# Asking for the last weight pieces earlier and splitting three of them on POOL, at the turn from gate products to position steps

## The chip, the cores and the metric

The program runs on one core of one Trainium2 chip. The metric is the device time of one execution in microseconds (us); less is better. The engines are named as in the profile: PE (TensorE matmul) with PEld (its weight loads), DVE (VectorE), ACT (ScalarE), POOL (GpSimd) and SP (SyncE, which here only issues DMAs).

## The reference

Two sequences, one of 2048 and one of 512 positions with 1024 channels, pass through the same trunk, all in float32:

```python
for layer in (attention, fourier):
    h = rmsnorm(x, g)
    # attention: o = banded grouped-query attention with sinks (|i-j| <= 128)
    # fourier:   f = Re(2-D FFT over (positions, 256 channels of a group)) of h
    x = x + (mixer(h) * silu(h @ w_gate)) @ w_out
y = rmsnorm(x, final_norm)
```

Only the second half of the Fourier layer matters here: the gate product `h @ w_gate`, the FFT over positions, the product with the gate, and the output product with `fourier_w_out`.

## The kernel before, in words

Every float32 product is made of three matmuls (`matmul3`, L92 to L94). Each operand is split into an upper part, rounded by an ACT cast, and a lower part, the difference, which an elementwise subtraction makes (`t[:, 1] = src - t[:, 0]`). L92 multiplies upper by upper, L93 upper of the left operand by lower of the right one, L94 lower by upper. So a weight piece is of use to L92 and L94 when ACT has cast it, and to L93 only when its lower part is there too.

`fourier_phase` runs first over ten pairs of 128-row tiles. For each pair `gates` makes the gate product by a scheme of sums: accumulators `W`, `Z` (two PSUM banks tagged `acc`) and `X`. `X` is made in four steps, `x_step(0)` to `x_step(3)`; each uses one 512 KB piece of the block B21 of the gate weights, and calls `more()`, which requests the next piece from DRAM (`b<-b21d`, L830). There are 40 pieces, two ahead at the start, so in the last pair `x_step(0)` requests the 39th piece and `x_step(1)` the 40th, which `x_step(3)` uses. Between the products, `hook(0)` to `hook(6)` run what the caller hands in.

For the last pair these hooks hold the way over to the second half. `f_load(k)` requests one of eight 512 KB pieces of the output weight (`w32f<-in_w_fout_dram`, L1118). `f_split(k)` makes two split tiles of it (`wo`, numbers 2k and 2k+1): ACT casts (L1124) and DVE subtracts (L1125). `position(...)` makes the FFT over positions: `gs` (or `gp`) parts by ACT L1027 and DVE L1028, matmuls into `As` and `Bs`, then ACT L1044 and L1048, DVE L1049, L1050 and the product with the gate rows `s2`, DVE L1052. `split_T` turns the result on PE (`tru`, L729), splits it by ACT L735 and DVE L736 into `tTu`. `finish` loads the residual rows (`x<-x1d`, L1063), makes two output halves of 24 matmuls each (`fo<-wo,tTu`), half 0 with `wo` 0 to 7 and half 1 with `wo` 8 to 15, adds them (DVE L1069), normalises (ACT L744, POOL L87, DVE L1081) and stores (L1082).

In the last pair the hooks run position 1 of the short sequence (`first`, two tiles, rows 2049 and 2051). After `gates` come positions 0 and 2 of it (`new`), then pieces 6 and 7 of the output weight, the splits of pieces 4 to 7, `finish` of the two tiles of `first`, and then the sixteen positions of the long sequence.

The text's order is not the order on the engines. A layer below records all operations, and orders them on each engine by a list scheduler; buffers come from pools (`left` has 20 places of 4 KB per partition, `xtile` four), and an operation that takes a place waits for the last use of it. Inside one engine's queue the order is fixed when the program is built, and a DMA whose wait is not over holds back all that follow on the same queue. `after(a, b)` adds an edge that keeps `a` behind `b` in the order, without a wait of its own. `tc.keep_in_program_order` keeps the ACT casts of `f_split` in the text's order.

Of the kernel before, what the change touches and what calls it, by code (L numbers as in the profile page):

```python
# [13 lines left out]
ALU = mybir.AluOpType  # L14
# [25 lines left out]
def f32(ap):  # L40
    return ap.bitcast(F32)
# [3 lines left out]
def encoder(  # L45
# [3 lines left out]
    PE, ACT, DVE, POOL, SP = nc.tensor, nc.scalar, nc.vector, nc.gpsimd, nc.sync  # L49
# [16 lines left out]
    x1d = dram.tile([T, D], F32, name="x1d")  # L66
# [8 lines left out]
    def bank(name):  # L75
        return psum.tile([P, 512], F32, tag="bank", name=name)

    def xtile(shape, dtype, name):
        return xp.tile(shape, dtype, align_bytes=LINE, tag="x", bufs=4, name=name)
# [10 lines left out]
    def matmul3(out, a, b, start, stop, more=False):  # L90

        PE.matmul(out, a[0], b[0], start=start, stop=False, skip_group_check=more)  # L92
        PE.matmul(out, a[0], b[1], start=False, stop=False, skip_group_check=more)  # L93
        PE.matmul(out, a[1], b[0], start=False, stop=stop, skip_group_check=more)  # L94
# [32 lines left out]
    def after(ins, anchor):  # L127

        if anchor is not None:
            tc.add_manual_dep(ins.ins, anchor.ins.name, ISSUE, reason="issue order")  # L130
# [565 lines left out]
    def fourier_phase(tail):  # L696
        with ExitStack() as es:
# [7 lines left out]
            def left(shape, dtype, name):  # L705
                return fp.tile(shape, dtype, align_bytes=LINE, tag="L", bufs=20, name=name)

            def right(shape, dtype, name):
                return zp.tile(shape, dtype, align_bytes=LINE, tag="R", bufs=16, name=name)
# [107 lines left out]
            def prod(out, a, b, ks, first):  # L817

                for k in ks:
                    cs = slice(k * P, (k + 1) * P)  # L820
                    matmul3(out, (a[0][:, cs], a[1][:, cs]), b[k], first and k == 0, k == 3, not first)
# [3 lines left out]
            def more():  # L825

                k = len(b21)
                if k < 4 * len(pairs):
                    t = right([P, 2, 512], F32R, f"b21_{k}")
                    SP.dma_start(f32(t), f32(b21d[k % 4]))  # L830
                    b21.append((t[:, 0], t[:, 1]))

            def gates(pr, hooks):

                n, A, S = pr.n, pr.A, pr.S
                W = psum2.tile([P, 512], F32, tag="acc", name=f"W{n}")
                Z = psum2.tile([P, 512], F32, tag="acc", name=f"Z{n}")
                X = bank(f"X{n}")

                def x_step(k):  # L840
                    prod(X, A[0, 1], b21[4 * n : 4 * n + 4], (k,), True)
                    more()

                def silu(c, i, half):
                    th = main.tile([P, 512], F32, tag="xr", bufs=3, name=f"gt{pr.ts[i]}_{half}")
                    ACT.activation(th, c, AF.Tanh, scale=0.5)
                    DVE.scalar_tensor_tensor(th, th, 1.0, c, ALU.add, ALU.mult)
                    t = pr.ts[i]
                    dst, t0 = (s2d[0], t) if t < SEQ // P else (s2d[1], t - SEQ // P)
                    POOL.dma_start(dst[t0 * P : (t0 + 1) * P, half * 512 : half * 512 + 512], th)  # L850

                def hook(i):
                    for h in hooks.get(i, ()):
                        h()

                four = range(4)
                c = xtile([P, 2, 512], F32, f"c{n}")
                c11, c22 = c[:, 0], c[:, 1]
                prod(W, A[0, 0], wg["B11"], four, True)
                ACT.copy(c11, W)  # L860
                hook(0)
                x_step(0)
                prod(Z, S[1], wg["T1"], four, True)
                ACT.copy(c22, Z)
                hook(1)
                prod(W, S[2], wg["T2"], four, False)
                c12 = fp.tile([P, 512], F32, tag="c12", bufs=1, name=f"c12_{n}")
                ACT.copy(c12, W)
                hook(2)
                x_step(1)  # L870
                prod(Z, S[4], wg["B22"], four, False)
                DVE.tensor_tensor(c12, c12, Z, ALU.add)
                silu(c12, 0, 1)
                hook(3)
                x_step(2)
                prod(W, S[3], wg["T3"], four, False)
                DVE.tensor_tensor(c22, c22, W, ALU.add)
                silu(c22, 1, 1)
                hook(4)
                x_step(3)  # L880
                DVE.tensor_tensor(c11, c11, X, ALU.add)
                silu(c11, 0, 0)
                hook(5)
                prod(W, A[1, 1], wg["N4"], four, False)
                silu(W, 1, 0)
                hook(6)
# [29 lines left out]
            def x_tile(name):  # L916
                return xtile([P, D], F32, name)

            order = [[16, 17, 18, 19]] + [[a, a + 4, a + 8, a + 12] for a in range(4)]
            pairs = [Pair(2 * gi + i // 2, tiles[i : i + 2]) for gi, tiles in enumerate(order) for i in (0, 2)]  # L920
# [3 lines left out]
            for i, s in enumerate(tail):  # L924
# [3 lines left out]
                if 1 <= i < 9:  # L928
                    w, k = split_steps[i - 1]
# [38 lines left out]
            pr = pairs[0]  # L968
# [23 lines left out]
            def rows(ap, r):  # L992
                return bass.AP(ap.tensor, ap.offset + r[0] * D, [[r[1] * D, P], [1, D]])
# [61 lines left out]
            def finish(uT, r, last=False):  # L1055
                r0 = r[0]
                dst, off = (y_prompt, 0) if r0 < SEQ else (y_sample, SEQ)
                out = rows(dst, (r0 - off, r[1]))
                if last:
                    ss = main.tile([P, 8], F32, tag="ss", bufs=2, name="ssl")  # L1060
                    junk = fp.tile([P, 512], F32, tag="c12", bufs=1, name="jkl").bitcast(BF16)
                x2 = x_tile(f"x2_{r0}")
                SP.dma_start(x2, rows(x1d, r))  # L1063
                for half in range(2):
                    ps = psum2.tile([P, 512], F32, tag="acc", name=f"fo{r0}_{half}")
                    for k in range(KD):
                        matmul3(ps, uT[k], wo[half * KD + k], k == 0, k == KD - 1)
                    xs = x2[:, half * 512 : half * 512 + 512]
                    DVE.tensor_tensor(xs, xs, ps, ALU.add)  # L1069
                    if last:  # L1070
                        ACT.activation(junk[:, :512], xs, AF.Square, accum_out=ss[:, half : half + 1])
                if last:
                    DVE.tensor_tensor(ss[:, 0:1], ss[:, 0:1], ss[:, 1:2], ALU.add)
                    inv = inv_rms(ss, 1, "invl")
                    for half in range(2):
                        hs = slice(half * 512, half * 512 + 512)
                        DVE.scalar_tensor_tensor(x2[:, hs], x2[:, hs], inv[:, 0:1], gfb[:, hs], ALU.mult, ALU.mult)
                        (SP, ACT)[half].dma_start(out[:, hs], x2[:, hs])
                    return
                inv = sumsq(x2, f"f{r0}")  # L1080
                DVE.scalar_tensor_tensor(x2, x2, inv[:, 0:1], gfb, ALU.mult, ALU.mult)  # L1081
                SP.dma_start(out, x2)  # L1082
# [28 lines left out]
                return name, 4 * k1, gl[0], gl[1] if len(gl) > 1 else None, tiles, (s2s, tb)  # L1111

            POOL.dma_start(mir, mirror)
            first, early, wo, w32f = [], [], [], []

            def f_load(k):
                w32f.append(left([P, 2, 512], F32, f"w32f{k}"))
                SP.dma_start(w32f[k].rearrange("p k c -> p (k c)"), w_fout[k // 4, k % 4])  # L1118

            def f_split(k):  # L1120
                for kk in range(2):
                    t = left([P, 2, 512], F32R, f"wo{2 * k + kk}")
                    src = w32f[k][:, kk]
                    tc.keep_in_program_order(ACT.copy(t[:, 0], src))  # L1124
                    DVE.tensor_tensor(t[:, 1], src, f32(t[:, 0]), ALU.subtract)  # L1125
                    wo.append((t[:, 0], t[:, 1]))

            def turn_first(i):
                u, r = first[i]
                pend.append((split_T(u, f"u{r[0]}", r[2] is not None), r))  # L1130
# [5 lines left out]
                2: [lambda: f_load(2), lambda: early.append(sample(2, (1,), (left,), (xtile,), left))],  # L1136
                3: [lambda: first.extend(position(*one)), lambda: f_load(3)],
                4: [lambda: f_split(0), lambda: f_split(1)],
                5: [lambda: turn_first(0), lambda: f_split(2), lambda: f_load(4)],
                6: [lambda: turn_first(1), lambda: f_split(3), lambda: f_load(5)],  # L1140
            })
            new = [t for p in early for t in position(*p)]
            for k in (6, 7):
                f_load(k)
            for k in range(4, 8):
                f_split(k)
            finish(*pend.pop(0))
            new = [(split_T(u, f"u{r[0]}", r[2] is not None), r) for u, r in new]
# [6 lines left out]
            for i, l in enumerate((w0, w2)):  # L1155
                for a in range(3):
                    t = zt(f"ev{a}_{i}")
# [31 lines left out]
            for a in range(4):  # L1189
                for i, l in enumerate((pc, qs)):  # L1190
# [3 lines left out]
                    t = zt(f"od{a}_{i}")  # L1194
# [127 lines left out]
```

## Time and profile before

| | us |
|---|---|
| three runs | 1663.11, 1664.00, 1667.96 |
| their median | 1664.00 |
| the profiled execution | 1665.56 |
| its span on the core | 1663.8 |
| PE busy in the span | 1640.0 (99%) |
| DVE, ACT, POOL busy | 1172.5, 873.8, 382.3 |
| granted TensorE clock, mean | 0.998 |

The profile's page lists busy time by engine, the span in slices, DMA queues, the chain that ended last, groups of instructions and DMA issues. Behind it stand answers of the trace: who waited for whom, the instructions in order of time, busy time by stretch. Times in them are us from the start of the span. A matmul of 512 columns is shown with 0.39 us, but the next one starts 0.23 us after it, since matmuls overlap; a PE that is shown busy may be far from its best. An arrow, as in `[1.94 <-DMA b<-b21d]`, gives the idle time before an instruction and what ended it. "SPq" is SP's queue of DMA issues.

### The profile page before, as it was taken

The numbers are of one execution on the slowest core, as the hardware profiler recorded it, in microseconds if no ns is written. First come the engines' busy times: TensorE is split into PE (matmuls) and PEld (weight loads), VectorE is DVE, ScalarE is ACT, GpSimd is POOL, SyncE is SP. The second block draws the span as 40 slices with busy tenths as digits, with TensorE's granted clock in tenths as the row PEclk, the third lists the DMA queues.
The fourth block names the chain that finished last, engine by engine and source line by source line (L and its number), as shares of the span: only waits on it lengthen the run. The fifth ranks groups of instructions, "written<-read, shape, count | busy, mean of one in ns | idle before, by whom it ended". The sixth has DMA issues, their size and how long they took to land.

```text
span 1663.8 us, 25654 instructions
## 1 busy us (share of the span) xinstructions
PE 1640.0 (99%) x8987; PEld 1410.4 (85%) x8987; DVE 1172.5 (70%) x2810; ACT 873.8 (53%) x1998; POOL 382.3 (23%) x536
## 2 busy tenths in 40 slices
PE   9999999999999999999999999999999999999997
PEld 7888788888898888988888888888888887888886
DVE  5787665888548886478874688768676769888553
ACT  6788644676236674256752466555554545342321
POOL 2465642112402113121122211221111111101000
PEclk9999999999999999999999999999999999999999
DMA  7486886454864456754549644556556578553331
GB/s 276 162 303 232 286 329 227 160 194 156 289 227 164 159 190 221 249 206 155 189 146 329 231 158 158 225 197 230 184 199 234 184 247 319 165 190 125 113 127 51
DMA packets 90252, 340.49 MB, mean 205 GB/s; under 512 B 11099, under 2 KB 21339, under 8 KB 72716
## 3 DMA queue, kind: packets, MB, share of 16 engines
q1 hardware_dynamic: 71676, 261.50, 46.0%
q0 software_dynamic: 18160, 76.56, 11.8%
q8 instruction: 72, 1.18, 0.3%
q10 hardware_dynamic: 288, 0.79, 0.1%
q14 instruction: 56, 0.46, 0.1%
HBM read 263.28 MB, written 75.53 MB: 204 GB/s over the span
## 4 chain that ended last, share of the span: by engine, by line
PE 82%; DVE 5%; ACT 5%; DMA 4%; issue 2%; POOL 1%; SPq 0%; DVEq 0%; POOLq 0%; ACTq 0%
PE spt L404 5%; PE av L457 5%; PE pt L443 5%; PE qp L92 4%; PE qp L94 4%; PE qp L93 4%; PE gp L92 4%; PE gp L94 4%; PE gp L93 4%; PE op L92 4%; PE op L94 3%; PE op L93 3%; PE fo L93 3%; PE fo L94 3%; PE fo L92 3%
## 5 line engine op out<-in xcount | busy, mean ns | idle before, releaser
L420 ACT ACTIVATE S<-S 128x385 f32<-128x385 f32 (+1 forms) x320 | 191.0, 597 | 46.8 <-DVE S L416 45.3
L444 ACT CAST pts<-pt 128x384 fp32r<-128x384 f32 (+1 forms) x320 | 144.2, 453 | 109.1 <-PE pt L443 104.5
L445 DVE TENSOR_TENSOR pts<-pt,pts 128x384 fp32r<-128x384 f32 (+1 forms) x320 | 168.3, 527 | 43.9 <-ACT pts L444 40.7
L416 DVE CUSTOM_DVE_ANT_0 S<-spt,b 128x385 f32<-128x385 f32 (+1 forms) x320 | 168.8, 528 | 34.7 <-PE spt L404 31.6
L404 PE MATMUL spt<-kwin,qab 128*128 128x384 f32 (+1 forms) x640 | 157.2, 327 | 1.1 <-DVE S L416 1.1
L476 POOL TENSOR_TENSOR o<-o,s 128x256 f32<-128x256 f32 x75 | 55.4, 739 | 437.7 <-DVE o L474 437.4
L443 PE MATMUL pt<-ident,S 128*128 128x128 f32 x896 | 150.6, 273 | 0.7 <-ACT S L429 0.6
L404 PEld LDWEIGHTS spt<-kwin,qab 128*128 128x128 f32 x640 | 118.2, 188 | 26.9 <-DVE S L416 1.7
L457 PEld LDWEIGHTS av<-pts,v 128*128 128x128 f32 x896 | 126.4, 189 | 14.0 <-DVE qab L353 1.6
L92 PE MATMUL gp<-h,wg 128*128 128x512 f32 x320 | 137.8, 431 | 0.0
L92 PE MATMUL qp<-h,wq 128*128 128x512 f32 x320 | 136.9, 428 | 0.8 <-DVE v L318 0.8
L457 PE MATMUL av<-pts,v 128*128 128x256 f32 x896 | 136.1, 285 | 1.4 <-DVE qab L353 1.1
L92 PE MATMUL op<-wo,uT 128*128 128x512 f32 x320 | 126.5, 397 | 1.5 <-ACT invb L165 0.8
L92 PE MATMUL fo<-wo,tTu 128*128 128x512 f32 x320 | 125.8, 393 | 1.3 <-ACT wo L1124 1.3
L443 PEld LDWEIGHTS pt<-ident,S 128*128 128x128 f32 x896 | 113.6, 140 | 15.7 <-DVE pts L445 3.2
L94 PE MATMUL qp<-h,wq 128*128 128x512 f32 x320 | 126.1, 394 | 0.0
L94 PE MATMUL gp<-h,wg 128*128 128x512 f32 x320 | 125.9, 393 | 0.0
L93 PE MATMUL op<-wo,uT 128*128 128x512 f32 x320 | 125.8, 393 | 0.0
L93 PE MATMUL qp<-h,wq 128*128 128x512 f32 x320 | 125.8, 393 | 0.0
L93 PE MATMUL gp<-h,wg 128*128 128x512 f32 x320 | 125.7, 393 | 0.0
L93 PE MATMUL fo<-wo,tTu 128*128 128x512 f32 x320 | 125.4, 392 | 0.1
L94 PE MATMUL fo<-wo,tTu 128*128 128x512 f32 x320 | 124.7, 390 | 0.0
(356 smaller groups left out, 4089.6 us busy)
## 6 DMA issues: line engine op xcount, KB each, us to landing
wo<-wsd SPq DMA_DIRECT2D x32, 1024.0 KB, 5.0
wq<-wsd SPq DMA_DIRECT2D x31, 1024.0 KB, 4.9
wg<-wsd SPq DMA_DIRECT2D x31, 1024.0 KB, 6.4
x<-x1d SPq DMA_DIRECT2D x40, 512.0 KB, 3.9
b<-b21d SPq DMA_DIRECT2D x40, 512.0 KB, 5.8
b<-rowd SPq DMA_DIRECT2D x40, 384.0 KB, 4.4
xs<-in_x_dram SPq DMA_DIRECT2D x23, 512.0 KB, 6.8
s2d<-gt POOLq DMA_DIRECT2D x40, 256.0 KB, 3.7
```

The costliest lines, as they stand in the source:

```text
L92: PE.matmul(out, a[0], b[0], start=start, stop=False, skip_group_check=more)
L93: PE.matmul(out, a[0], b[1], start=False, stop=False, skip_group_check=more)
L94: PE.matmul(out, a[1], b[0], start=False, stop=stop, skip_group_check=more)
L404: PE.matmul(ps[:, 2 + k0 * P : 2 + k1 * P], q, kwin[g][:, part, b * P + k0 * P : b * P + k1 * P], start=part == 0, stop=part == 1,)
L416: DVE.tensor_tensor_reduce(out=s[:, e0:e1], in0=ps[:, 1 + e0 : 1 + e1], in1=st["bias"][:, j, 386 - e1 : 386 - e0][:, ::-1], scale=1.0, sca ...
L420: last_exp[0] = ACT.activation(s[:, e0:e1], s[:, e0:e1], AF.Exp, bias=mn, scale=-1.0, accum_out=den)
L443: PE.transpose(ps[:, kb, :], s[:, 1 + kb * P : 1 + (kb + 1) * P], ident)
L444: ACT.copy(hi[:, k0:k1, j, :], ps[:, k0:k1, :])
L445: DVE.tensor_tensor(lo[:, k0:k1, j, :], ps[:, k0:k1, :], f32(hi[:, k0:k1, j, :]), ALU.subtract)
L457: PE.matmul(out, v, pt[:, kb].rearrange("p h q -> p (h q)"), start=kb == k0 and part == 0, stop=kb == k1 - 1 and part == 1,)
L476: eng.tensor_tensor(o, o, s, ALU.mult)
```

## The change

The 40th B21 piece is requested by an extra `more()` in the last pair, right behind `x_step(0)`. Piece 5 of the output weight is requested in hook 5, with piece 4; pieces 4 and 5 are split in hook 6, and pieces 6 and 7 are each split behind their own load. The residual loads of `finish` are kept behind the last requested output weight piece. The lower parts of pieces 5, 6 and 7 are made on POOL, in two halves of 256 columns: twelve POOL instructions in place of six DVE ones of 512 columns. Nothing else differs.

```diff
@@ gates @@
                 hook(0)
                 x_step(0)
+                if pr is pairs[-1]:
+
+                    more()
                 prod(Z, S[1], wg["T1"], four, True)
@@ finish @@
                 x2 = x_tile(f"x2_{r0}")
-                SP.dma_start(x2, rows(x1d, r))
+                after(SP.dma_start(x2, rows(x1d, r)), loaded[0])
@@ fourier_phase @@
-            first, early, wo, w32f = [], [], [], []
+            first, early, wo, w32f, loaded = [], [], [], [], [None]
 
             def f_load(k):
                 w32f.append(left([P, 2, 512], F32, f"w32f{k}"))
-                SP.dma_start(w32f[k].rearrange("p k c -> p (k c)"), w_fout[k // 4, k % 4])
+                loaded[0] = SP.dma_start(w32f[k].rearrange("p k c -> p (k c)"), w_fout[k // 4, k % 4])
 
             def f_split(k):
                 for kk in range(2):
                     t = left([P, 2, 512], F32R, f"wo{2 * k + kk}")
                     src = w32f[k][:, kk]
                     tc.keep_in_program_order(ACT.copy(t[:, 0], src))
-                    DVE.tensor_tensor(t[:, 1], src, f32(t[:, 0]), ALU.subtract)
+                    for cs in (slice(0, 256), slice(256, 512)) if k > 4 else (slice(0, 512),):
+
+                        (POOL if k > 4 else DVE).tensor_tensor(t[:, 1, cs], src[:, cs], f32(t[:, 0, cs]), ALU.subtract)
                     wo.append((t[:, 0], t[:, 1]))
...
                 4: [lambda: f_split(0), lambda: f_split(1)],
-                5: [lambda: turn_first(0), lambda: f_split(2), lambda: f_load(4)],
-                6: [lambda: turn_first(1), lambda: f_split(3), lambda: f_load(5)],
+                5: [lambda: turn_first(0), lambda: f_split(2), lambda: f_load(4), lambda: f_load(5)],
+                6: [lambda: turn_first(1), lambda: f_split(3), lambda: f_split(4), lambda: f_split(5)],
             })
             new = [t for p in early for t in position(*p)]
             for k in (6, 7):
                 f_load(k)
-            for k in range(4, 8):
                 f_split(k)
             finish(*pend.pop(0))
```

## The prediction

> **What bounds the kernel now.** I read the page first, then the waits, the order of time and the DMA landings of the turn, and last how DVE and POOL meet elsewhere in the run. PE carries the end: 99% busy, 82% of the chain that ended last. Its line:
>
> ```profile
> PE 1640.0 (99%) x8987; PEld 1410.4 (85%) x8987; DVE 1172.5 (70%) x2810; ACT 873.8 (53%) x1998; POOL 382.3 (23%) x536
> ```
>
> So only what PE loses counts. Busy time by stretch shows where: PE is idle 1.94 of 5 us, 1.53 of 8 and 0.51 of 9, and not at all before and after.
>
> ```profile
> 1360.00:1378.00 18.00, 18.00 (x94) 15.41 (x93) 10.57 (x14) 4.67 (x11) 3.64 (x5) 1.00 0.97 355
> 1378.00:1383.00 5.00, 3.06 (x20) 2.37 (x19) 4.46 (x8) 0.64 (x2) 0.00 (x0) 1.00 0.76 260
> ...
> 1390.00:1398.00 8.00, 6.47 (x31) 4.42 (x29) 7.75 (x15) 5.20 (x15) 0.54 (x1) 1.00 0.98 378
> 1398.00:1407.00 9.00, 8.49 (x44) 6.66 (x45) 9.00 (x16) 5.18 (x10) 2.13 (x4) 1.00 1.04 413
> 1407.00:1418.00 11.00, 11.00 (x50) 8.98 (x49) 10.70 (x13) 2.42 (x5) 0.57 (x1) 1.00 0.65 232
> ```
>
> Busy flatters PE here, since an interrupted matmul shows its whole length. By starts, the stage's work is 64 matmuls of 512 columns at 0.2275 us, 24 of 256 or 260 at 0.12 and 32 turns at 0.106: 20.8 us. It takes from 1378.82 to 1407.10, so 7.5 us are lost, and no change of this stage can gain more.
>
> In order of time, the first loss is X's last step, which waits for the 40th B21 piece; the largest of the others is the first matmul of half 1, which waits for ACT's cast of `wo` 8:
>
> ```profile
> 1378.59 0.39 PE L94 MATMUL W<-wT,S 128*128 128x512 f32 x1
> 1380.92 0.50 PE L92 MATMUL X<-b,tTb 128*128 128x512 f32 x1 [1.94 <-DMA b<-b21d]
> ...
> 1398.04 0.50 PE L92 MATMUL fo<-wo,tTu 128*128 128x512 f32 x1 [1.25 <-ACT wo L1124]
> ```
>
> SP issued that piece at 1367.61, ninth of a row of ten loads, and it landed 13.26 us later. Piece 4 of the output weight left only at 1380.45 and pieces 5 to 7 at 1388.63, each behind a residual load.
>
> ```profile
> 1367.61 0.50 SPq L830 DMA_DIRECT2D b<-b21d  x1
> 1368.21 0.41 SPq L1118 DMA_DIRECT2D w32f<-in_w_fout_dram  x1
> 1380.04 0.32 SPq L1063 DMA_DIRECT2D x<-x1d  x1
> 1380.45 0.38 SPq L1118 DMA_DIRECT2D w32f<-in_w_fout_dram  x1
> 1388.21 0.32 SPq L1063 DMA_DIRECT2D x<-x1d  x1
> 1388.63 1.37 SPq L1118 DMA_DIRECT2D w32f<-in_w_fout_dram  x3
> ```
>
> **Part 1, the B21 piece.** In the built program it is SP's second load of the row, after piece 0 (1361.79), and waits for PE's `X` with piece 37, which ends at 1363.8. Held behind it are piece 1, a `gsd` row tile and a gate row tile: 1.9 us later than now at first (1362.47 before), caught up by 1368. The loads of one queue land in order here (1366.5, 1370.0, 1372.4, ... 1382.1), so this one lands near 1368 and the others at most 1.9 us later than now; the earliest needed of them, pieces 0 and 1, are cast from 1383. Cost nothing. If that cover went, a late piece 1 would cost what it is late, under 2 us.
>
> X then runs from 1378.82 to 1379.50. What is late next is DVE: `us<-us,s2s` for row 2049 ends at 1380.01, for row 2051 at 1381.15, and L877, for which the next `W` matmul waits, at 1381.75. So `tru` goes from 1380.12 and `W` starts at 1381.93, against 1383.17 now. **Gain 1.24 us**, not the 2.1 us of the wait.
>
> **Part 2, pieces 4 and 5.** The residual loads no longer stand ahead: 4 and 5 wait for piece 39 or 1 to land and for PE's Z, near 1371.5, leave there and land by about 1385 behind the row. Pieces 6 and 7 now take the places of pieces 2 and 4, and wait for DVE's lower parts of `wo` 5 (1388.6) and 9 (1392.8 or a little more); with some 4.8 us to landing (piece 4 at 1380.45 took that on a short queue) they are there by 1393.5 and 1398.5. Both residual loads and four `evd` loads queue behind piece 7; the residuals land by about 1401, used at 1405. Nothing.
>
> ACT's casts of 8 to 11 now stand among the `gs` casts. Everything on ACT starts 1.37 us sooner (L846 at 1382.42), and at 0.52 us a cast `wo` 10 ends at 1391.82 and the last `gs` at 1392.87. PE gets `wo` 8 at 1390.3 in place of 1398.0, but waits 0.3 to 0.8 us each for the casts of `gs`. DVE, continuous at 0.605 us per 512 columns, reaches lower `wo` 8 at 1391.54 and 9 at 1392.14.
>
> **Part 3, twelve subtractions on POOL.** The same form exists:
>
> ```profile
> L118 POOL TENSOR_TENSOR wo<-w32o,wo 128x256 fp32r<-128x256 f32 x32 | 22.7, 738 | 8.5 <-ACT wo L113 8.5
> ```
>
> At 0.70 us from start to start, four halves of a piece take 2.83 us, against 1.28 on DVE. If POOL worked alone, adding up the queues gives: `wo` 10 and 11 done at 1394.9, just as PE comes; `wo` 12 cast at 1397.44, PE at its L93 from 1397.76 but POOL done at 1399.0 (wait 1.3), `wo` 13 at 1400.5 (0.8), `wo` 14 cast at 1403.2 behind two `tTu` casts (0.9), DVE's residual sum (0.4), lower 14 (0.4) and 15 (0.8). The first matmul behind them, L93 of the second `fo` tile, starts at 1406.74, against 1407.10 now: −0.36 us. PE's waits for POOL eat 3.3 us, nearly all that parts 1 and 2 bring.
>
> But POOL does not work alone. DVE instructions that read two tensors from SBUF wait for it:
>
> ```profile
> 213.84 0.75 DVE L187 SCALAR_TENSOR_TENSOR h<-xk,g0s,h 128x512 fp32r<-128x512 f32 x1 [0.24 <-ACT h L186]
> 215.08 0.64 DVE L195 SCALAR_TENSOR_TENSOR hl<-xk,g0s,hl 128x128 fp32r<-128x128 f32 x1 [0.49 <-ACT hl L194]
> 220.02 4.94 DVE L187 SCALAR_TENSOR_TENSOR h<-xk,g0s,h 128x512 fp32r<-128x512 f32 x1 [4.30 <-ACT h L186]
> ```
> ```profile
> 214.84 2.87 POOL L118 TENSOR_TENSOR wo<-w32o,wo 128x256 fp32r<-128x256 f32 x4 [0.72 <-ACT wo L113]
> ...
> 219.77 4.63 POOL L182 TENSOR_TENSOR xk<-xk,invb 128x640 f32<-128x640 f32 x3
> ```
>
> L187 takes 0.75 us alone and 4.94 where three POOL products follow each other: it ends 0.55 us after the third. L195 (0.34 alone) took 0.64 beside the first 256-column half and slipped in before the second. L445, with one operand in PSUM, takes 554 ns with and without POOL. In the new places, `wo` 10 and 11 meet DVE's lower `wo` 9 and four lower `gs` (all two SBUF tensors), and `wo` 12 and 13 meet the two `us<-us,s2s` that the next turns wait for. `wo` 14 and 15 meet L736 and L1069, which read PSUM: nothing.
>
> By L195's row, the nearest in POOL's shape, they take turns: a POOL half and then a DVE instruction, some 1.10 us a pair, so 0.5 us more for DVE per half. An estimate from these rows: four halves put the last lower `gs` from 1395.2 to 1397.2, PE reaches `wo` 12 at 1399.2 in place of 1397.5, and of `wo` 12 and 13, POOL's second pair waits for the two products, so that L93 of `wo` 13 starts at 1403.8. Turns, casts and `wo` 14, 15 follow as above, and the matmul that is now at 1407.10 starts at 1409.9: **+2.8 us**. If POOL keeps its turn between 12 and 13, 1408.7 (+1.6). If DVE is shut out for whole chains, as at 220.02, the first two chains are paid in full: −0.36 + 2 × 2.83 = +5.3. I take the middle, the row with POOL's shape.
>
> [...]
>
> **Behind the stage** PE has no idle time until 1450 and DVE is 97% busy, so nothing absorbs a shift. The store of row 2049 now precedes two gate row loads on SP; they land near 1420, used at 1428. Nothing.
>
> **Rivals.**
> *No meeting*: POOL and DVE overlap freely, −0.4 us. For: L445. Against: L187, 4.94 us on three occasions. Not slower than before; it decides if lower `gs` stays at 0.68 us.
> *DVE shut out for whole chains*: +5.3 us, for and against as above. It decides if one DVE instruction near 1393 lasts over 2.5 us.
> *PE's waits all go*: at best −7.5 us; over 5 us only if POOL's halves are early everywhere, which its 2.83 us a piece against PE's 1.37 us of matmuls per piece speaks against.
>
> **How the numbers follow.** The profiled execution took 1665.56 us, 1.56 above the median of 1664.00; its sum gives 1668.4, and the median 1664.0 + 2.8 = 1666.8. About 0.3%, 5 us, is what a measurement of this kernel can tell from no change. Chances: taking turns (+1.6 to +4) 0.54, no meeting 0.18, shut out 0.23, all waits gone 0.05. The first two are within 0.3%, the third over it, the fourth faster: 0.05, 0.72, 0.23. Range: from no meeting (1663.6) less its largest wait for POOL, 1.3 us, should that not arise, and less the 0.9 us by which the lowest run lies below the median, 1661.4, to shut out plus 1.5 us for chains that also delay each other, 1670.8.
>
> **What would show it.** X's wait for `b<-b21d` gone and `W` on N4 about 1.2 us sooner after X's `W`; no wait for the cast of `wo` 8; PE waiting for POOL `wo` at L93 four times, most for `wo` 13; POOL's halves at 0.73 us, and L1028 and L1052 of DVE stretched by 0.4 us or more wherever a half runs. Wrong if L1028 keeps 0.68 us (then −0.4), if one is stretched over 2.5 us, or if X still waits.

## The result, and the profile after

The changed kernel took 1669.45 us, median of 12 runs (1667.92 to 1671.91), the kernel before 1665.47 us in the same session (12 runs). The ratio is 1.0023, 95% interval [1.0015, 1.0030]: 3.8 us slower, between 2.5 and 5.0. The forecast was 2.8 us slower, 1666.8 against a median of 1664.0.

The profiled execution took 1667.93 us. First the busy line of its page, and busy time by stretch. The changed execution entered the stage 0.81 us sooner (the entry varies by that much between profiles: the first `tru` behind X starts at 1379.58 in run 1's, at 1378.51 in run 2's), so its stretches are laid 0.8 us sooner than those of before.

```profile
PE 1640.3 (98%) x8987; PEld 1410.5 (85%) x8987; DVE 1168.1 (70%) x2804; ACT 873.3 (52%) x1998; POOL 396.2 (24%) x548
```
```profile
1377.20:1382.20 5.00, 4.43 (x27) 3.45 (x26) 4.93 (x8) 2.13 (x5) 0.00 (x0) 1.00 0.97 395
...
1389.20:1397.20 8.00, 6.07 (x32) 4.59 (x31) 5.96 (x11) 4.76 (x13) 6.00 (x5) 1.00 0.96 328
1397.20:1406.20 9.00, 5.02 (x29) 3.72 (x29) 6.41 (x11) 3.44 (x8) 5.46 (x6) 1.00 0.93 356
```

In the first stretch PE now idles 0.57 us, not 1.94. In the next two it idles 1.93 and 3.98, where it was 1.53 and 0.51. POOL, which had next to nothing to do there, is busy 6.0 and 5.5 us, for the most part with eight of its twelve halves, which by the old row take 0.74 us each.

PE in order of time:

```profile
1378.01 0.39 PE L92 MATMUL X<-b,tTb 128*128 128x512 f32 x1
...
1381.09 0.48 PE L92 MATMUL W<-wN,tTb 128*128 128x512 f32 x1
...
1389.52 0.49 PE L92 MATMUL fo<-wo,tTu 128*128 128x512 f32 x1
...
1395.74 0.50 PE L93 MATMUL fo<-wo,tTu 128*128 128x512 f32 x1 [1.32 <-POOL wo L1130]
...
1399.79 0.51 PE L93 MATMUL fo<-wo,tTu 128*128 128x512 f32 x1 [0.93 <-POOL wo L1130]
...
1403.12 0.50 PE L93 MATMUL fo<-wo,tTu 128*128 128x512 f32 x1 [2.35 <-POOL wo L1130]
...
1405.96 0.50 PE L92 MATMUL fo<-wo,tTu 128*128 128x512 f32 x1 [0.70 <-ACT wo L1127]
```

X no longer waits, `wo` 8 (1389.52) no longer waits for its cast, and the waits for POOL are those for `wo` 10, 12 and 13. The fourth, 0.41 us for `wo` 15, follows at 1408.86. A wait for the cast of `wo` 14 is new too.

To compare whole traces, matmuls of the two were matched one by one by operation and tiles, and their starts subtracted. From 1250 to the last `W` ahead of X the changed one is 0.81 us ahead; from 1418 to 1470 it is 2.53 us behind. **So this stage costs 3.34 us more.** This number, "the shift over the stage", is given for every run below. Behind 1490 it is 2.01 behind: 0.52 us came back. Net, that is 2.83 us.

### The profile page after: what moved, and what is told of

Same layout as the page of the kernel before. It is cut to its first block, busy times and chain, and to the rows that moved or that the text cites. A ratio compares the mean times of both kernels' runs of the same rounds, so it can differ in the third digit from the quotient of the medians.

```text
span 1665.8 us, 25654 instructions
## 1 busy us (share of the span) xinstructions
PE 1640.3 (98%) x8987; PEld 1410.5 (85%) x8987; DVE 1168.1 (70%) x2804; ACT 873.3 (52%) x1998; POOL 396.2 (24%) x548
## 3 DMA queue, kind: packets, MB, share of 16 engines
q8 instruction: 72, 1.18, 0.3%
## 4 chain that ended last, share of the span: by engine, by line
PE 83%; ACT 4%; DVE 4%; DMA 3%; issue 3%; POOL 3%; POOLq 0%; SPq 0%; DVEq 0%; ACTq 0%
PE spt L404 5%; PE av L457 5%; PE pt L443 5%; PE qp L92 4%; PE qp L94 4%; PE qp L93 4%; PE gp L92 4%; PE gp L94 4%; PE gp L93 4%; PE op L92 4%; PE op L94 3%; PE op L93 3%; PE fo L93 3%; PE fo L94 3%; PE fo L92 3%
## 5 line engine op out<-in xcount | busy, mean ns | idle before, releaser
L93 PE MATMUL fo<-wo,tTu 128*128 128x512 f32 x320 | 125.4, 392 | 5.1 <-POOL wo L1130 5.0
L92 PE MATMUL op<-wo,uT 128*128 128x512 f32 x320 | 126.5, 397 | 1.6 <-ACT invb L165 0.8
L92 PE MATMUL fo<-wo,tTu 128*128 128x512 f32 x320 | 125.9, 393 | 0.8 <-ACT wo L1127 0.7
L93 PE MATMUL op<-wo,uT 128*128 128x512 f32 x320 | 125.8, 393 | 0.0
L93 PE MATMUL qp<-h,wq 128*128 128x512 f32 x320 | 125.7, 393 | 0.0
L93 PE MATMUL gp<-h,wg 128*128 128x512 f32 x320 | 125.7, 393 | 0.0
L94 PE MATMUL op<-wo,uT 128*128 128x512 f32 x320 | 124.7, 391 | 0.0
```

## The experiments

For each run the table gives the ratio against the kernel before (medians of 10 to 12 runs, of 5 for POOL's lower parts alone) and, from its one profile, the shift over the stage. "Half clock" is the time in the stage in which the granted TensorE clock was 0.50; what it is shows in the ninth run.

| run | ratio, 95% interval | shift over the stage | half clock |
|---|---|---|---|
| the changed kernel | 1.0023 [1.0015, 1.0030] | +3.34 | 0 |
| all lower parts on DVE | 0.9995 [0.9986, 1.0004] | +1.32 | 6.8 |
| POOL, 512 columns at once | 1.0008 [1.0000, 1.0017] | +2.37 | 3.4 |
| the B21 piece alone | 0.9996 [0.9987, 1.0004] | −0.51 | 3.4 |
| POOL's lower parts alone | 1.0044 [1.0030, 1.0058] | +7.75 | 6.8 |
| changed, no lower gs | 1.0004 [0.9994, 1.0013] | +0.29 | 0 |
| changed, no us\*s2s | 1.0014 [1.0005, 1.0024] | +1.83 | 0 |
| requests alone, DVE | 0.9991 [0.9982, 1.0000] | −0.45 | 3.4 |
| piece 4 split early, DVE | 1.0003 [0.9994, 1.0012] | +0.54 | 3.4 |
| only casts of 8, 9 early, DVE | 1.0000 [0.9990, 1.0010] | +0.55 | 3.4 |
| only casts of 8 to 11 early, DVE | 1.0001 [0.9990, 1.0011] | +0.39 | 3.4 |
| requests, last piece on POOL | 1.0003 [0.9993, 1.0012] | +0.93 | 0 |
| changed, piece 5 on DVE | 1.0014 [1.0005, 1.0023] | +3.55 | 3.4 |

A microsecond is 0.0006 of the ratio. In run 9 matmuls of 512 columns start every 0.43 us at half clock, in place of 0.23. An estimate from these two numbers: a stretch of it can hold up to half its length of lost time, so shifts with 3.4 in the last column may be up to 1.7 us too high, and those with 6.8 up to 3.4.

**1. All lower parts on DVE.**

```diff
-                    for cs in (slice(0, 256), slice(256, 512)) if k > 4 else (slice(0, 512),):
-                        (POOL if k > 4 else DVE).tensor_tensor(t[:, 1, cs], src[:, cs], f32(t[:, 0, cs]), ALU.subtract)
+                    for cs in (slice(0, 256), slice(256, 512)) if k > 7 else (slice(0, 512),):
+                        (POOL if k > 7 else DVE).tensor_tensor(t[:, 1, cs], src[:, cs], f32(t[:, 0, cs]), ALU.subtract)
```

> The changed kernel with the lower parts of all eight pieces on DVE, 512 columns each, as before the change; the earlier requests, the earlier splits and the orders of SP and ACT stay. The planner then puts the lower parts of wo 10 and 11 on DVE ahead of the four lower gs, 12 between the two products us*s2s and 13 to 15 behind them. Theory A (the price of the change is POOL and DVE meeting, the earlier requests bring 1.2 us and more): the shift of PE over this stage falls from +3.3 us to between -1 and 0, total 3 to 4 us below the changed kernel. Theory B (the price is the new order of PE, ACT and DVE, whoever makes the lower parts): the four lower gs come 1.2 us later, wo 12 waits for DVE until 1401.2 in place of 1399.7, and the shift stays at +2 to +3.3, total at most 1.3 us below the changed kernel.

The ratio is 0.0028 below that of the changed kernel, 4.7 us, where theory A had 3 to 4 and theory B at most 1.3. The shift, +1.32, lies between their ranges, but 6.8 us of this profile's stage ran at half clock. So POOL's use is what makes the change slow. That the requests and early splits bring something by themselves is not shown: the interval of 0.9995 includes 1.

**2. POOL in one piece.**

```diff
-                    for cs in (slice(0, 256), slice(256, 512)) if k > 4 else (slice(0, 512),):
+                    for cs in (slice(0, 512),):
```

> The changed kernel with each lower part on POOL as one instruction of 512 columns (some 1.4 us) in place of two halves; the order of all other instructions is the same. Theory P (DVE goes first: POOL waits until DVE has no instruction with two SBUF operands at hand, and DVE waits only for the POOL instruction that already runs): the first one still ends 1.4 us behind DVE's last lower gs, the four lower gs keep 0.60 us a step, only us*s2s waits up to 0.7 us more; total within 1 us of the changed kernel. Theory T (they take turns, one POOL instruction and then one DVE instruction, as the prediction had it): each DVE instruction beside POOL waits 1.4 us, the last lower gs comes some 2 us later, total 2 us or more above the changed kernel.

Neither fits: the shift is 1 us lower than with halves, the ratio 0.0015, about 2.5 us, lower. The four lower gs kept 0.60 us a step, as theory P said, and the first POOL instruction ended 1.13 us behind the end of the last of them, so turns are out at this place. In the meeting with us\*s2s, POOL was done sooner:

```profile
1397.34 3.48 POOL L1130 TENSOR_TENSOR wo<-w32f,wo 128x512 fp32r<-128x512 f32 x2 [1.39 <-ACT wo L1127]
```

Two instructions of 512 columns took 3.48 us there, four of 256 take 4.75 in the changed kernel: one wait of 0.97 us behind a DVE product in place of two. (Alone, 512 columns take 1.28 us, two halves 1.41.) Cutting POOL's work into halves made it later here, not sooner.

**3. The B21 piece alone.**

```diff
                 x_step(0)
+                if pr is pairs[-1]:
+                    more()
                 prod(Z, S[1], wg["T1"], four, True)
```

> The kernel before with only the extra request of the 40th B21 piece; everything behind keeps its order. If the prediction's step for this part holds, X's last step no longer waits (1.94 us before) and the next W matmul starts 1.24 us sooner behind it; of this the stage keeps 0.3 to 1.24 us, since pieces 4 to 7 of the output weight still leave behind the residual loads: total 0.3 to 1.2 us below the kernel before. Rival: all of it is given back, because wo 8 is cast behind ACT's copies as before and PE waits there 1.2 us longer: total unchanged within 0.3 us.

X's wait is gone, and 1.26 us of waiting for the cast of `wo` 8 stays. The shift says that at least 0.51 of the 1.24 us is kept; the ratio, 0.9996, can't tell it from nothing.

**4. POOL's lower parts alone**, in the kernel before, with requests and splits where they were:

```diff
-                    DVE.tensor_tensor(t[:, 1], src, f32(t[:, 0]), ALU.subtract)
+                    for cs in (slice(0, 256), slice(256, 512)) if k > 4 else (slice(0, 512),):
+                        (POOL if k > 4 else DVE).tensor_tensor(t[:, 1, cs], src[:, cs], f32(t[:, 0, cs]), ALU.subtract)
```

> The kernel before with only the lower parts of pieces 5, 6 and 7 on POOL in two halves each; requests and splits stay where they were, so POOL's twelve halves all come behind the casts of wo 8 to 15 from 1397.4 on. Theory P (DVE first): the first half waits for DVE's lower wo 8 and 9, until 1400.1; wo 11 is done near 1404, 13 near 1407, 15 near 1410; total 3 to 6 us above the kernel before. Theory T (turns): DVE's two lower parts and the products us*s2s each wait for a half, POOL is done about 1 us sooner; 2 to 5 us above. If POOL's parts cost nothing by themselves: within 0.5 us of the kernel before.

7.3 us slower, above both ranges, though the interval (5.0 to 9.7) reaches into them. One detail speaks against P: POOL's first half did not wait for both of DVE's lower `wo` 8 and 9, but ran between them (end at 1397.81, then lower 9 until 1398.36). So DVE doesn't go first everywhere. And behind PE's waits for POOL, 1.32 and 2.43 us, PE ran at half clock for 6.8 us, which no theory had priced.

**5. and 6. The meetings taken away.** The first leaves out the four lower gs (their L93 products take the upper part), the second the two products us\*s2s.

```diff
-                            DVE.tensor_tensor(t[:, 1], gv, f32(t[:, 0]), ALU.subtract)
+                            if name not in ("s0", "s2"):
+                                DVE.tensor_tensor(t[:, 1], gv, f32(t[:, 0]), ALU.subtract)
...
-                                t[:, part].rearrange("p (g c) -> p g c", g=2)[:, :, c0 : c0 + n]
+                                t[:, part if name not in ("s0", "s2") else 0].rearrange("p (g c) -> p g c", g=2)[:, :, c0 : c0 + n]
```

> The changed kernel without the four lower parts gs of positions 0 and 2 of the short sequence; their L93 products take the upper part once more. So POOL's first pieces meet only DVE's lower wo 9. Theory P (POOL had to wait for DVE's whole run of wo 9 and four gs, 3.2 us): wo 10 and 11 are done by 1394.9, PE's wait of 1.32 us for wo 10 is gone, and the shift of PE over the stage falls from +3.34 us by 1.0 to 1.6 us, to about +2.0. Rival (POOL's late start is covered, the order of PE's own instructions is the price): the shift stays within 0.5 us of +3.34, with the time lost again at the next wait.

```diff
                 for u, s2 in zip(us, s2s):
-                    DVE.tensor_tensor(u, u, s2, ALU.mult)
+                    if name not in ("s0", "s2"):
+                        DVE.tensor_tensor(u, u, s2, ALU.mult)
```

> The changed kernel without the two products us*s2s of rows 2048 and 2050 (us goes to the turns as it is). So wo 12 and 13 on POOL meet nothing of DVE that reads two tensors from SBUF. If the two halves of 1.70 us in place of 0.73 are the price, wo 13 is done 1.9 us sooner, PE's wait of 2.35 us for it falls to 0.3 to 0.7 us, and the shift over the stage falls from +3.34 us to between +1.2 and +1.8. Together with the run without the lower gs that makes 3 us of the 3.34. Rival (the turns wait for something else behind it, the casts of wo 14 and tTu on ACT): the shift falls by less than 0.8 us.

Neither profile has half clock in the stage. Without the products the shift is +1.83, at the upper end of what was expected, and PE's wait for `wo` 13 is 0.41. Without the lower gs it is +0.29, far lower than expected. POOL in that run:

```profile
1391.35 3.56 POOL L1131 TENSOR_TENSOR wo<-w32f,wo 128x256 fp32r<-128x256 f32 x4 [1.89 <-ACT wo L1128]
1396.03 3.08 POOL L1131 TENSOR_TENSOR wo<-w32f,wo 128x256 fp32r<-128x256 f32 x4 [1.12 <-ACT wo L1128]
```

The first chain waits 0.75 us, for lower `wo` 9 only, in place of 3.16: the 2.41 us between are the four lower gs at 0.60. And the second chain, sooner, is through in 3.08 us in place of 4.75, since it now meets the end of one product only. So this run takes away both meetings, and the two gains (3.05 and 1.51) may not be added. The meetings account for at most 3.05 of the 3.34 us; how much of that is the 2.4 us of work which this run also spares DVE is not separated.

**7. and 8. What is split early.** Requests as in the changed kernel, all lower parts on DVE, and pieces 4 to 7 split behind the gate stage (7), or piece 4 with piece 3 (8):

```diff
-                6: [lambda: turn_first(1), lambda: f_split(3), lambda: f_split(4), lambda: f_split(5)],
+                6: [lambda: turn_first(1), lambda: f_split(3)],                                # 7
+                6: [lambda: turn_first(1), lambda: f_split(3), lambda: f_split(4)],            # 8
```

> The changed kernel with its earlier requests, but pieces 4 to 7 are split behind the gate stage as in the kernel before, and all lower parts are on DVE. If the earlier splits of pieces 4 and 5 are what costs 1.3 us with all lower parts on DVE, this one has the shift of the run with the B21 piece alone, -0.5 us, give or take 0.4. If the requests themselves cost (the residual loads and gate rows behind them), the shift is above 0. If the late pieces were what the stage waited for, it is under -1.2.

> As the run before it, but piece 4 (wo 8 and 9) is split with piece 3, as in the changed kernel; pieces 5 to 7 behind the gate stage, all on DVE. PE's wait of 1.26 us for the cast of wo 8 must go. DVE makes lower wo 8 and 9 ahead of the four lower gs, which then come 1.2 us later. If PE has enough of wo 8 and 9 to cover that, the shift is -0.8 to -1.8 us, below both kernels; if the positions bound the stage (their gs, As, us, turn, one behind the other), it is 0 to +1.0, on the way to the +1.32 of the run with pieces 4 and 5 split early.

−0.45 and +0.54, both with one stretch of half clock. The first is what was expected: sooner requests of pieces 4 to 7 bring nothing beyond the B21 piece. It is also the best ratio, 0.9991, whose interval ends at 1. In the second, PE's wait for the cast of `wo` 8 went, and waits of 0.76 us for the cast of a later tile and of 1.81 us for us\*s2s took its place: the positions bound this part (gs, `As`, us, product, turn, one behind the other), and what is put ahead of their lower gs delays the turns.

**9. and 10. Casts early, lower parts late.** `f_split` is divided; only ACT's casts of `wo` 8 and 9 (9), or of 8 to 11 (10), stand in hook 6.

```diff
-                6: [lambda: turn_first(1), lambda: f_split(3)],
+                6: [lambda: turn_first(1), lambda: f_split(3), lambda: f_cast(4)],                       # 9
+                6: [lambda: turn_first(1), lambda: f_split(3), lambda: f_cast(4), lambda: f_cast(5)],    # 10
```

> As the run with the requests alone (all lower parts on DVE, pieces 4 to 7 split behind the gate stage), but ACT casts wo 8 and 9 already in hook 6; their lower parts stay where they were, and DVE's order does not change. PE's wait of 1.25 us for the cast of wo 8 must go, and its first matmul of half 1 moves ahead among the As products. If that cast was what PE waited for, the shift over the stage goes from -0.45 to between -1.2 and -1.7 us. If DVE's chain (gs, us, us*s2s, then lower wo 8, without a gap) bounds the stage, PE waits for us*s2s and for lower wo 8 in its place: -0.4 to -0.8 us. A shift above 0 would say that two casts among the gs casts alone cost what splitting piece 4 early did (+0.54).

> As the run before it, with the casts of wo 8 to 11 in hook 6. DVE's order now has all four lower gs ahead of the first us, and lower wo 8 to 15 behind the products, so PE's turns come ahead of its fo products, as in the run with all on DVE (+1.32). If the order of PE that the planner draws from such casts is what costs, the shift is +0.3 to +1.3 us though DVE has no more to do ahead of the positions; if only DVE's lower parts ahead of gs cost, it is below 0.

+0.55 and +0.39, each with one stretch of half clock, as run 7 has at −0.45: ACT counts as much as DVE. Two casts among the gs casts put the first product us\*s2s 1.0 us later than in run 7, counted from the entry into the stage. In run 9 PE then waits for it, with nothing left to do, and this is what follows (the wait, then busy time by stretch with the clock ahead of the DMA share):

```profile
1396.24 0.63 PE L729 MATMUL tru<-ident,us 128*128 128x128 f32 x4 [2.61 <-DVE us L1055]
```
```profile
1393.50:1396.20 2.70, 0.12 (x2) 0.00 (x0) 2.15 (x5) 2.34 (x7) 0.00 (x0) 1.00 1.02 408
...
1397.40:1400.40 3.00, 3.00 (x12) 2.33 (x10) 3.00 (x6) 1.25 (x3) 0.54 (x1) 0.53 1.02 416
```

The matmuls of 512 columns from 1398.12 on start every 0.43 us in place of 0.23. That lasts 3.4 us, as in every profile of the table that has it once; in two it lasts twice that.

**11. The last piece on POOL**, in run 7's kernel:

```diff
-                    for cs in (slice(0, 256), slice(256, 512)) if k > 7 else (slice(0, 512),):
-                        (POOL if k > 7 else DVE).tensor_tensor(t[:, 1, cs], src[:, cs], f32(t[:, 0, cs]), ALU.subtract)
+                    for cs in (slice(0, 256), slice(256, 512)) if k > 6 else (slice(0, 512),):
+                        (POOL if k > 6 else DVE).tensor_tensor(t[:, 1, cs], src[:, cs], f32(t[:, 0, cs]), ALU.subtract)
```

> As the run with the requests alone, but the lower parts of the last piece only (wo 14 and 15) on POOL in halves, behind all others. [...] If POOL is free help for a busy DVE, DVE ends 1.2 us sooner and the shift falls to -0.6 to -1.6 us.

+0.93, without half clock; run 7 has −0.45 with it. Here the two engines meet in the open. DVE and POOL in order of time:

```profile
1399.60 1.76 DVE L1055 TENSOR_TENSOR us<-us,s2s 128x1024 f32<-128x1024 f32 x1
1401.28 3.50 DVE L1130 TENSOR_TENSOR wo<-w32f,wo 128x512 fp32r<-128x512 f32 x3
```
```profile
1399.52 4.71 POOL L1130 TENSOR_TENSOR wo<-w32f,wo 128x256 fp32r<-128x256 f32 x4
```

Three lower parts that take 1.88 us in a row elsewhere take 3.50: one starts every 1.14 us. Two more on POOL's side, 1.18 us each in place of 0.74, lie exactly between them. That is taking turns, with the 1.10 us a pair of the prediction. POOL as help took 1.2 us off DVE (two times 0.60) and put 2.2 us on it as waits (0.54 on the product, 0.54 on each of the three).

**12. Only pieces 6 and 7 on POOL.**

```diff
-                    for cs in (slice(0, 256), slice(256, 512)) if k > 4 else (slice(0, 512),):
-                        (POOL if k > 4 else DVE).tensor_tensor(t[:, 1, cs], src[:, cs], f32(t[:, 0, cs]), ALU.subtract)
+                    for cs in (slice(0, 256), slice(256, 512)) if k > 5 else (slice(0, 512),):
+                        (POOL if k > 5 else DVE).tensor_tensor(t[:, 1, cs], src[:, cs], f32(t[:, 0, cs]), ALU.subtract)
```

> The changed kernel with the lower parts of piece 5 (wo 10 and 11) on DVE and only those of pieces 6 and 7 on POOL: so POOL never meets the run of lower wo and gs, and meets only the two products us*s2s. If the second meeting is most of POOL's price (the run without these products took off 1.5 us, and the wait for wo 13 was the longest), the shift over the stage stays at +2.6 to +3.3 us against +1.32 with all on DVE. If the first meeting is (POOL kept out for 3.2 us, PE's wait of 1.32 us), the shift falls to +1.3 to +2.0 us.

+3.55 with one stretch of half clock, so 1.85 to 3.55, which reaches into both ranges. By the ratios this run is 3.2 us slower than the one with all on DVE, and the changed kernel 4.7 us, each give or take 2. The longest wait is unchanged:

```profile
1405.51 0.80 PE L93 MATMUL fo<-wo,tTu 128*128 128x512 f32 x1 [2.37 <-POOL wo L1130]
```

So the second meeting, with us\*s2s, seems to carry the larger part of POOL's price; the ratios and this wait point that way, and the shift alone can't settle it. Taking away the first one alone is not a gain that the shift shows: its work, back on DVE, pushes the lower gs 1.2 us back.

## Why the prediction was right, and where it was not

**Part 1 held.** `W` on N4 starts 3.31 us behind the last `W` matmul ahead of X's last step; it was 4.58. Gain 1.27 us, forecast 1.24. The piece was issued as the program's order said:

```profile
1363.02 0.32 SPq L830 DMA_DIRECT2D b<-b21d  x1
```

It landed at 1369.90, 8 us before its use. With 0.81 us added for the entry, as in all times below that stand beside a forecast, that is 1370.71 (forecast near 1368). **Part 2 held in its times**: `wo` 8 runs at 1390.33 (forecast 1390.3), the last gs cast ends at 1392.9 (1392.87), and both residuals land before 1400 (1401). What part 2 is worth was not forecast apart from part 3, and runs 8 to 10 show why it is little: casts and lower parts ahead of gs delay the turns.

**Part 3: the meeting was there, but in the first place the other engine paid.** The lines of the changed kernel, POOL and then DVE; the last POOL line is an answer for a shorter stretch, the first half alone:

```profile
1391.11 5.96 POOL L1130 TENSOR_TENSOR wo<-w32f,wo 128x256 fp32r<-128x256 f32 x4 [1.87 <-ACT wo L1127]
1398.32 4.75 POOL L1130 TENSOR_TENSOR wo<-w32f,wo 128x256 fp32r<-128x256 f32 x4 [1.24 <-ACT wo L1127]
...
1406.00 2.80 POOL L1130 TENSOR_TENSOR wo<-w32f,wo 128x256 fp32r<-128x256 f32 x4 [2.42 <-ACT wo L1127]
```
```profile
1391.11 3.89 POOL L1130 TENSOR_TENSOR wo<-w32f,wo 128x256 fp32r<-128x256 f32 x1 [1.87 <-ACT wo L1127]
```
```profile
1391.93 2.49 DVE L1031 TENSOR_TENSOR gs<-gl,gs 128x512 fp32r<-128x512 f32 x4
...
1399.07 1.75 DVE L1055 TENSOR_TENSOR us<-us,s2s 128x1024 f32<-128x1024 f32 x1
...
1401.18 1.30 DVE L1055 TENSOR_TENSOR us<-us,s2s 128x1024 f32<-128x1024 f32 x1
```

The third chain meets nothing and takes 2.80 us, the bound that the prediction had. The step that failed is "0.5 us more for DVE per half" at the first chain: the four lower gs took 2.49 us, not stretched at all, and POOL's first half took 3.89 in place of 0.73. It waited until DVE's run was over. By the prediction's own sign, lower gs at 0.68 us, there should have been no meeting and −0.36 us; the sign was wrong, because it looked for the cost on DVE alone. The total came out nevertheless, since PE waits for the later of the two: the forecast had the last lower gs at up to 1397.2 and `wo` 12 reached at 1399.2; measured are a last lower gs at 1395.22, `wo` 11 from POOL at 1397.88, and `wo` 12 reached at 1399.28. That the two delays come out alike is luck.

At the second chain the forecast held as it stood: the products took 1.75 and 1.30 us (1.22 alone), two POOL halves 1.70, and L93 of `wo` 13 started at 1403.93, forecast 1403.8. The waits for `wo` 14's cast and `wo` 15 were 0.70 and 0.41 (0.9 and 0.8 forecast). The matmul that was at 1407.10 comes at 1410.44, forecast 1409.9: of the 0.5 us too few, 0.1 are there at `wo` 13, and where the rest arises behind it was not followed.

**That the total fits so well is in part luck.** The stage costs 3.34 us, not 2.8. In the kernel before, PE waited 0.47 us for a lower gp at 1474.05, and in the changed trace it does not, so the net of the two profiles is 2.83. That does not show that something there absorbs a shift: 0.2 to 0.8 us come back at this place in all 13 other profiles, also in those of runs 3 and 7, whose stage was faster than before. So the 0.5 us looks like a loss of the one profile of the kernel before, and "nothing absorbs a shift" may well hold. The runs say 3.8, with both 2.8 and 3.34 inside their interval.

**The rivals.** "No meeting" was half right by its sign and wrong in time. "Shut out for whole chains" did happen, with the roles reversed: POOL was shut out, for 3.16 us, and lost about 1.3 us of PE's time by it.

In run 11 and at the second chain the waits were 0.4 to 1.0 us, at most one instruction long. At the first chain POOL waited 3.16 us, five DVE instructions long. What decides between the two is open, and what the engines wait for at a meeting is not shown either. DVE's instructions followed without a gap in both cases, and in run 4 POOL got in between two of them. One difference stands in the traces: in all four kernels in which POOL was kept out to the end of DVE's run (the changed one and runs 2, 5 and 6), it came during the third instruction of that run, and in run 4 during the first. No run was made to separate the causes.

## What to carry to other kernels

A second engine is not always free help: where DVE and POOL both read two tensors from SBUF, they waited for each other here, 0.4 to 3.16 us at a time. A lower part took 0.60 us on DVE and 1.41 on POOL, and in run 11 DVE's started every 1.14 us, with a POOL half between two of them, so work moved from a busy DVE to POOL came back as waits. Where DVE read PSUM there was no stretch: beside the third chain, itself 2.80 us, L1072 took 0.68 us and two of L736 1.29, against 0.68 and 1.28 in the kernel before. Look for the loss on both sides of a meeting, and hand POOL long instructions there, not halves (run 2). And before pulling work forward, find the chain that the consumer waits for: casts and subtractions of `wo` that went ahead of gs, on either engine, came back as a wait for us\*s2s.

## What the hardware showed that was not expected

In 9 of the 14 profiles of this stage PE's granted clock fell to 0.50, each time for 3.4 us or twice that, behind or within waits of PE of 1.2 to 2.6 us; matmuls of 512 columns then started every 0.43 us in run 9, in place of 0.23. Not every such wait did it: the changed kernel's profile has one of 2.35 us and the kernel before one of 1.94, both at 1.00 throughout, and runs 7 and 11 have the same waits up to 1397 (1.25 and 0.22 us), one with a stretch of half clock behind them, one without. So a wait of PE can have a price behind it that a sum of waits does not see, up to 1.7 us for each 3.4 us of half clock by the estimate above, and one profile of a kernel is no measure of it. What decides whether half clock follows a wait is not shown: no run was made to test it.
